# RWKV recurrence on TensorE: output products grouped by their shape, heads alternating in the products within chunks

## The chip, the cores and the metric

The kernel runs on one core of one Trainium2 chip. The metric is the device time of one execution in microseconds; the median of three runs is given. A core has five engines that matter here: TensorE (PE, whose weight loads are listed apart as PEld), VectorE (DVE), ScalarE (ACT), GpSimd (POOL) and SyncE (SP), which issues DMAs. TensorE multiplies a stationary operand (rows x columns of its 128x128 array) with a moving operand and writes into PSUM.

## The reference

Two transformer stacks of two layers each run one after the other on a sequence of 256 tokens of width 1024. The change is inside the first mixer of the second stack, the RWKV-7 recurrence, which has 8 heads of 64 channels:

```python
def step(state, inp):
    r_t, w_t, k_t, v_t, kk_t, a_t = inp
    sa = jnp.einsum('bhij,bhj->bhi', state, -kk_t)
    state = (state * w_t[:, :, None, :] + sa[..., None] * (kk_t * a_t)[:, :, None, :]
             + v_t[..., None] * k_t[:, :, None, :])
    return state, jnp.einsum('bhij,bhj->bhi', state, r_t)
...
_, y = lax.scan(step, state0, (tm(r), tm(decay), tm(k), tm(v), tm(kk), tm(a)))
```

The state of a head is 64x64. Beside the recurrence stands a stick-breaking attention of 8 heads on the same input; the outputs of both go into one product with `w_out`.

## The kernel before

All activations stand transposed, channels on partitions and the 256 tokens along the free side. Weights stream from HBM in 399 chunks of 128x1024 through four raw buffers; ACT makes a high part of a chunk (L418) and DVE a low part (L419), and every product with weights is three matmuls (helper at L385, as are nearly all others, so tiles and not lines tell them apart).

The recurrence is not run token by token. The 256 tokens are four chunks c of 64. The 8 heads are four pairs j, and e says which half of the 128 partitions a head of a pair has. Ahead of the chunks, `gp(j)` makes the products of one pair within all chunks: for each e and c a stationary operand of 64 rows x 128 columns from `BK` and a moving one of 128 columns from `KR`, into one PSUM tile for each e. DVE masks the results into `GR` (what a token's output takes from earlier tokens of its chunk) and `GB`. `am` makes the matrices that `invl`, `invc` and `invs` invert: the matrices go through DRAM (tiles dA, dY, dZ), DVE does 15 short rows of the inversion, and `lw_`, `ly`, `lz` finish it on PE.

Then the chunks follow one another, each with four steps:

- `ck(c)`: from chunk 1 on, 8 products of 64x64 quarters of the array, `KR` with the state `S0`; DVE adds them up (L1314).
- `ct(c)`: 8 products of quarters; ACT and DVE copy them into `SV` (L1321, L1322).
- `cs_(c)`: 8 products of 128 rows x 64 columns; DVE makes the next state `S1` (L1332, L1333).
- `cy(c)`: the output. For each of 8 heads one product of `SV` and `GR` over 128 rows and 64 columns, and, from chunk 1 on, one product of a 64x64 quarter, `S0` with `KR`, that is added to it. All go into one PSUM tile of the pool "o"; ACT copies it out (L1348).

These are float32 products; the trace shows two passes on PE for each, so 8 products stand there as x16. Which step stands where on PE is written out by hand in HYB_ORDER, and PE keeps that order. Between the steps of the chunks it has steps of the attention: `sz` (scores), `sp` (transposes at L783 and products with the values), `gt` (gate), `gn` and `gv` (norm of the output). Around them:

```python
cs_.0 cy.0 jv.1 ck.1 sp.0 ct.1 gt.2 sz.2.0 cs_.1 cy.1 sz.2.1 ck.2 sp.1 ct.2 sz.3.0 gn.0 cs_.2 gt.1 sz.3.1 cy.2
ck.3 sp.2 ct.3 gt.3 gv.0 cy.3 sp.3 gvf.0
```

This is HYB_ORDER from the end of chunk 0 on. The order on DVE, ACT, POOL and SP is not written by hand: a scheduler sets it when the program is built, from the order in which the instructions are written and its own estimate of when each is ready. PSUM tiles come by turns from the pools "s" and "t", two buffers each; "o" has one.

Of the kernel before, what the change touches and what calls it, by code (L numbers as in the profile page):

```python
# [20 lines left out]
P = 128  # L21
# [302 lines left out]
class Net:  # L324
# [685 lines left out]
    def hybrid_body(self, p, X):  # L1010
# [10 lines left out]
        half = lambda e: slice(64 * e, 64 * e + 64)  # L1021
# [24 lines left out]
        for i, x in enumerate((dY, dZ)):  # L1046
            y = x.rearrange("t e a b -> (t e) (a b)")
            for k in range(2):
                nc.sync.dma_start(out=y[:, k * 512:k * 512 + 512], in_=zero)
        SV = one("SV", P, 4, 4, 2, 64)  # L1050
        RW0 = 1536
        R = dict(kx={}, rx={}, vx={}, gl={}, qa={}, kv={}, kr={}, vr={}, ENL={}, TA={}, KP={}, KR={}, BK={}, GR={}, GB={},
                 MA={}, Y={}, Y2={}, Z={}, W={}, G1={}, BG={}, bo={}, BV={}, BT={}, ST={}, YC={}, OB={}, out={}, ps={}, ps2={})
# [117 lines left out]
        def gp(j):  # L1171
            KR, BK = R["KR"][j], R["BK"][j]
            gb = c64(f1())
            gm = lambda o: cst["gmask"][:, o:o + 64].unsqueeze(1).to_broadcast([P, 4, 64])
            for e in range(2):
                ps = self.pa([P, 4, P])
                for c in range(4):
                    self.mm(ps[:, c], BK[half(e), c, e:e + 2], KR[half(e), c])
                gr = self.t(p, [P, 4, 64], "GR", bufs=8)
                v.tensor_tensor(gr, ps[:, :, 64:128], gm(64), ALU.mult)  # L1180
                r2 = half(1 - e)
                v.tensor_tensor(gb[r2], ps[r2, :, 0:64], gm(0)[r2], ALU.mult)
                R["GR"][j, e] = gr
            R["GB"][j] = gb
# [116 lines left out]
        each = [(j, e) for j in range(4) for e in range(2)]  # L1301
# [36 lines left out]
        def cy(c):  # L1338
            if c == 0:
                R["y"] = [b2(2, S) for _ in range(2)]  # L1340
            yps = self.po([P, 4, 64])
            for j, e in each:
                o = yps[half(e), j]
                self.mm(o, SV[:, j, c, e], R["GR"][j, e][:, c], stop=c == 0)
                if c:
                    self.mm(o, R["S0"][half(e), j], R["KR"][j][half(e), c, 1], start=False)
            for q in range(2):
                a.copy(R["y"][q][:, :, c * 64:c * 64 + 64], yps[:, 2 * q:2 * q + 2])  # L1348
            R["S0"] = R["S1"]
# [376 lines left out]
```

## Time and profile before

| | us |
|---|---|
| median of 3 runs | 1318.56 |
| lowest and highest run | 1316.29, 1318.71 |
| profiled execution | 1321.39 |
| its span, first instruction to last | 1319.6 |
| PE busy | 1292.5 (98%) |
| PEld busy | 1231.4 (93%) |
| DVE busy | 1026.5 (78%) |
| ACT busy | 781.9 (59%) |
| steps gp (first to last product) | 626 to 657 |
| chunks 1 to 3, with the steps between them | 703 to 751 |

Busy time of PE is modelled at the end of each matmul, so that a busy PE need not be at its peak; how fast it goes is read from the distance between the starts of two groups of the timeline. A group there is a run of alike instructions: start, length, engine, line, operation, out<-in by the program's names, the part of the array (rows*columns), the moving operand's shape, and how many. Idle time of the engine before a group stands in brackets, with what ended it.

### The profile page before, as it was taken

The page shows a single profiled execution, that of the slowest core. Times are in us where ns is not written, and L with a number is a line of the kernel's source. Part 1 is how long each engine was busy: PE and PEld are TensorE (multiplying, and loading weights), DVE is VectorE, ACT ScalarE, POOL GpSimd, SP SyncE. Part 2 cuts the span into 40 slices and gives each one's busy share as a digit, 9 for nine tenths or more (in the row PEclk, how much of TensorE's full clock was granted, in tenths as well). Part 3 has the DMA queues.
Part 4 walks back from the last instruction along what each step waited for, and adds up shares of the span by engine and source line. Part 5 has one row for each costly group of instructions (what it writes and reads, how often), then busy time and mean ns, then how long its engine had stood idle before and what let it go on. Part 6 is the DMA issues. An engine that isn't in the chain of part 4 may idle for free.

```text
span 1319.6 us, 27125 instructions
## 1 busy us (share of the span) xinstructions
PE 1292.5 (98%) x10864; PEld 1231.4 (93%) x10864; DVE 1026.5 (78%) x2037; ACT 781.9 (59%) x1359; POOL 16.1 (1%) x48
## 2 busy tenths in 40 slices
PE   7999999999999999999999999999999999999997
PEld 5999999988899999999876799999998989999997
DVE  5889997566679998578964488897779978889656
ACT  6667665457667665448343266665557766665544
POOL 0000000000000000001100000000000000000000
PEclk9999999999999999999998799999999999999998
DMA  7566555555446556574440056565555436665551
GB/s 271 176 225 193 189 189 182 189 187 177 132 145 192 191 180 190 191 237 145 124 129 18 17 167 206 192 190 182 189 176 161 127 113 189 193 198 181 191 182 60
DMA packets 70398, 223.18 MB, mean 169 GB/s; under 512 B 13408, under 2 KB 15712, under 8 KB 70272
## 3 DMA queue, kind: packets, MB, share of 16 engines
q1 hardware_dynamic: 63312, 212.43, 50.3%
q10 hardware_dynamic: 6192, 5.34, 1.4%
q0 software_dynamic: 768, 3.67, 0.8%
q8 instruction: 85, 1.39, 0.4%
q14 instruction: 41, 0.34, 0.1%
HBM read 218.53 MB, written 2.88 MB: 168 GB/s over the span
## 4 chain that ended last, share of the span: by engine, by line
PE 92%; DVE 4%; DMA 2%; ACT 1%; issue 1%; SPq 0%; ACTq 0%; DVEq 0%
PE g L385 78%; PE s L385 6%; PE t L385 3%; PE o L385 3%; PE t L783 1%; DVE wlo L419 1%; DMA raw<-in_wall 0%; DMA b<-dZ 0%; DVE tm L1217 0%; ACT whi L418 0%; DMA dA<-b 0%; DVE sqa L171 0%; DVE xl L497 0%; DVE tm L1219 0%; DMA tm<-dA 0%
## 5 line engine op out<-in xcount | busy, mean ns | idle before, releaser
L385 PE MATMUL g<-xh,whi 128*128 128x256 f32 x2184 | 618.0, 283 | 1.4 <-ACT xh L496 1.4
L385 PE MATMUL g<-xl,whi 128*128 128x256 f32 x2184 | 610.3, 279 | 2.5 <-DVE xl L497 2.4
L419 DVE TENSOR_TENSOR wlo<-raw,whi 128x1024 fp32r<-128x1024 f32 (+1 forms) x400 | 487.8, 1221 | 160.4 <-ACT whi L418 157.4
L418 ACT ACTIVATE whi<-raw 128x1024 fp32r<-128x1024 f32 (+1 forms) x400 | 421.9, 1055 | 317.4 <-PE g L385 172.5
L385 PE MATMUL g<-xh,wlo 128*128 128x256 f32 x2184 | 609.6, 279 | 0.1
L385 PEld LDWEIGHTS g<-xh,whi 128*128 128x128 f32 x2184 | 410.7, 188 | 7.2 <-issue 4.0
L385 PEld LDWEIGHTS g<-xl,whi 128*128 128x128 f32 x2184 | 410.9, 188 | 4.0 <-DVE xl L497 3.3
L385 PEld LDWEIGHTS g<-xh,wlo 128*128 128x128 f32 x2184 | 414.1, 190 | 0.3 <-DVE wlo L419 0.3
L385 PE MATMUL g<-hh,wlo 128*128 128x256 f32 x704 | 197.8, 281 | 0.0
L385 PE MATMUL g<-hl,whi 128*128 128x256 f32 x704 | 197.8, 281 | 0.0
L385 PE MATMUL g<-hh,whi 128*128 128x256 f32 x704 | 197.8, 281 | 0.0
L385 PEld LDWEIGHTS g<-hh,wlo 128*128 128x128 f32 x704 | 135.2, 192 | 0.0
L385 PEld LDWEIGHTS g<-hh,whi 128*128 128x128 f32 x704 | 132.2, 188 | 0.0
L385 PEld LDWEIGHTS g<-hl,whi 128*128 128x128 f32 x704 | 132.2, 188 | 0.0
L277 ACT ACTIVATE hh<-pr 128x256 fp32r<-128x256 f32 x88 | 36.0, 409 | 48.7 <-DVE pr L272 48.7
L496 ACT ACTIVATE xh<-h,vec 128x256 fp32r<-128x256 f32 x80 | 39.1, 499 | 24.0 <-DVE h L560 20.9
L867 ACT ACTIVATE c<-pad,vec 128x256 f32<-128x256 f32 x88 | 47.7, 590 | 9.4 <-DVE pad L856 9.4
L874 DVE SCALAR_TENSOR_TENSOR c<-pad,vec,c 128x256 f32<-128x256 f32 x88 | 42.7, 485 | 3.1
L497 DVE SCALAR_TENSOR_TENSOR xl<-h,vec,xh 128x256 fp32r<-128x256 f32 x80 | 37.9, 481 | 6.9 <-ACT xh L496 6.8
L872 DVE SCALAR_TENSOR_TENSOR c<-pad,vec,c 128x256 f32<-128x256 f32 x88 | 42.2, 480 | 0.0
L282 DVE TENSOR_TENSOR hl<-pr,hh 128x256 fp32r<-128x256 f32 x88 | 36.9, 420 | 3.9 <-ACT hh L277 3.9
L385 PE MATMUL g<-whi,xh 128*128 128x512 f32 x68 | 29.1, 428 | 9.2 <-ACT xh L496 9.2
(375 smaller groups left out, 1396.1 us busy)
## 6 DMA issues: line engine op xcount, KB each, us to landing
raw<-in_wall SPq DMA_DIRECT2D x398, 512.0 KB, 3.5
bias<-in_bias POOLq DMA_DIRECT2D x4, 768.0 KB, 7.1
cst_c<-in_c ACTq DMA_DIRECT2D x1, 896.0 KB, 7.1
raw<-in_wall SPq DMA_DIRECT2D x2, 256.0 KB, 4.1
h<-in_x ACTq DMA_DIRECT2D x2, 256.0 KB, 4.3
h<-in_x POOLq DMA_DIRECT2D x2, 256.0 KB, 7.6
ws<-in_ws ACTq DMA_DIRECT2D x1, 512.0 KB, 8.7
bs<-in_bs ACTq DMA_DIRECT2D x1, 512.0 KB, 8.8
```

The lines of the kernel that those rows point to most:

```text
L277: self.net.nc.scalar.activation(self.H[-1][0], self.pr, AF.Copy)
L282: self.net.nc.vector.tensor_tensor(hl, self.pr, hh.bitcast(F32), ALU.subtract)
L385: self.nc.tensor.matmul(out, lhsT=lhsT, rhs=rhs, start=start, stop=stop, skip_group_check=True)
L418: nc.scalar.activation(hi[:, s], raw[:, s], AF.Copy)
L419: self.after(nc.vector.tensor_tensor(lo[:, s], raw[:, s], hi[:, s].bitcast(F32), ALU.subtract))
L496: self.nc.scalar.activation(xh, h, AF.Copy, scale=gain)
L497: self.nc.vector.scalar_tensor_tensor(xl, h, gain, xh.bitcast(F32), ALU.mult, ALU.subtract)
L783: self.nc.tensor.transpose(pt[:, b * P:b * P + P], w[:, s * P:s * P + P], self.cst["ident"])
L867: a.activation(c0, pad[:, j, 2:], AF.Identity, bias=self.col("f_conv_b", (l,), j * KF + i), scale=cw(2, j))
L872: v.scalar_tensor_tensor(c1, pad[:, j, 1:S + 1], cw(1, j), cc[n], ALU.mult, ALU.add)
L874: v.scalar_tensor_tensor(cc[n], pad[:, j, 0:S], cw(0, j), c1, ALU.mult, ALU.add)
```

## The change

Two places of the RWKV step are written in another order. Every product of before is there after, with the same operands and the same size.

In `gp`, both PSUM tiles of a pair are taken first, and within a chunk c the products of both heads e follow one another; before, the four products of one head came first and the four of the other second. The two heads' stationary operands lie in different halves of the array's rows.

In `cy`, the 8 products of 128 rows come first, and then, from chunk 1 on, the 8 quarter products; before, each quarter product stood right behind its head's product of 128 rows. Since only the first write of a bank now carries the start flag, `start` is set for j = 0 alone.

```diff
-            for e in range(2):
-                ps = self.pa([P, 4, P])
-                for c in range(4):
-                    self.mm(ps[:, c], BK[half(e), c, e:e + 2], KR[half(e), c])
+            both = [self.pa([P, 4, P]) for _ in range(2)]
+            for c in range(4):
+                for e in range(2):
+                    self.mm(both[e][:, c], BK[half(e), c, e:e + 2], KR[half(e), c])
+            for e, ps in enumerate(both):
                 gr = self.t(p, [P, 4, 64], "GR", bufs=8)
...
             yps = self.po([P, 4, 64])
+
             for j, e in each:
-                o = yps[half(e), j]
-                self.mm(o, SV[:, j, c, e], R["GR"][j, e][:, c], stop=c == 0)
-                if c:
-                    self.mm(o, R["S0"][half(e), j], R["KR"][j][half(e), c, 1], start=False)
+                self.mm(yps[half(e), j], SV[:, j, c, e], R["GR"][j, e][:, c], start=j == 0, stop=c == 0)
+            for j, e in each if c else ():
+                self.mm(yps[half(e), j], R["S0"][half(e), j], R["KR"][j][half(e), c, 1], start=False)
```

On PE, the output of chunk 1 (`cy.1`) began like this before. GR with SV is a product of 128 rows, b (a `KR`) with tm (the state) a quarter product; the numbers tell tiles apart.

```order
L385 MATMUL s_9614<-SV_7880,BK_9075 64x64 x4
L385 MATMUL o_9627<-GR_8619,SV_7880 64x64
L385 MATMUL o_9627<-b_8453,tm_9532 64x64
L385 MATMUL o_9627<-GR_8627,SV_7880 64x64
L385 MATMUL o_9627<-b_8453,tm_9532 64x64
L385 MATMUL o_9627<-GR_8956,SV_7880 64x64
L385 MATMUL o_9627<-b_8380,tm_9532 64x64
L385 MATMUL o_9627<-GR_8964,SV_7880 64x64
```

The same place of the changed kernel, to its end and to the score products that follow:

```order
L385 MATMUL o_9627<-GR_8624,SV_7880 64x64
L385 MATMUL o_9627<-GR_8627,SV_7880 64x64
L385 MATMUL o_9627<-GR_8961,SV_7880 64x64
L385 MATMUL o_9627<-GR_8964,SV_7880 64x64
L385 MATMUL o_9627<-GR_8729,SV_7880 64x64
L385 MATMUL o_9627<-GR_8732,SV_7880 64x64
L385 MATMUL o_9627<-GR_8779,SV_7880 64x64
L385 MATMUL o_9627<-GR_8782,SV_7880 64x64
L385 MATMUL o_9627<-b_8453,tm_9532 64x64 x2
L385 MATMUL o_9627<-b_8380,tm_9532 64x64 x2
L385 MATMUL o_9627<-b_8549,tm_9532 64x64 x2
L385 MATMUL o_9627<-b_8568,tm_9532 64x64 x2
```

What alternated 15 times between the two shapes is now two runs of 8; `cy.2` and `cy.3` read alike. `cy.0`, which has no quarter products, is as before.

PE at the first of the four `gp` steps: a head's four products follow each other before, and the heads (tiles t and s) alternate now.

```order
 L385 MATMUL g_8468<-xh_7823,wlo_8471 128x256
-L385 MATMUL t_8614<-b_8453,BK_8454 128x128 x4
-L385 MATMUL s_8622<-b_8453,BK_8454 128x128 x4
+L385 MATMUL t_8614<-b_8453,BK_8454 128x128
+L385 MATMUL s_8615<-b_8453,BK_8454 128x128
+L385 MATMUL t_8614<-b_8453,BK_8454 128x128
+L385 MATMUL s_8615<-b_8453,BK_8454 128x128
```

The scheduler also puts a few instructions of DVE and ACT in another order between the `gp` steps and the end of the inversion. DVE at the end of the inversion's 15 rows (the reduction of 128x15 is the last of them; the copy at L1220 makes what goes to dZ), before:

```order
L1219 TENSOR_REDUCE tm_8816<-tm_8818 128x15
L419 TENSOR_TENSOR wlo_8925<-raw_8923,whi_8924 128x1024
L1220 COPY tm_8817<-tm_8816 128x256
L1308 COPY tm_9376<-b_8907 128x128
L1267 TENSOR_TENSOR f_8948<-t_8946,f_8432 128x256
```

and after (lines from `gp` to `cy` have one number more):

```order
L1220 TENSOR_REDUCE tm_8816<-tm_8818 128x15
L1221 COPY tm_8817<-tm_8816 128x256
L1309 COPY tm_9376<-b_8907 128x128
L419 TENSOR_TENSOR wlo_8925<-raw_8923,whi_8924 128x1024
L1268 TENSOR_TENSOR f_8948<-t_8946,f_8432 128x256
```

The low part of a weight chunk moved from before that copy to behind it. POOL and SP have the order of before.

## Rows read from the trace of the kernel before

**Rows 1.** The page, part 2: granted TensorE clock in 40 slices of 33 us, tenths.

```profile
PEclk9999999999999999999998799999999999999998
```

**Rows 2.** The chain of work that ended last, 590 to 770 us: start, us, what.

```profile
709.72 4.10 PE o L385 x32
...
742.71 5.62 PE o L385 x32
```

**Rows 3.** Timeline of PE, cy.0 to the start of cy.1: start, us, instructions.

```profile
701.45 0.64 PE L385 MATMUL o<-GR,SV 128*64 128x64 f32 x16
702.01 1.12 PE L385 MATMUL s<-b,cst_c 128*128 128x512 f32 x2
...
703.07 0.68 PE L385 MATMUL t<-tm,b 64*64 64x64 f32 x16
703.68 0.55 PE L783 MATMUL t<-cst_c,st 128*128 128x128 f32 x3
...
706.32 0.68 PE L385 MATMUL s<-tm,b 64*64 64x64 f32 x16
706.93 1.32 PE L385 MATMUL t<-sg,b 128*128 128x256 f32 x4
708.18 0.92 PE L385 MATMUL s<-f,f 64*128 64x128 f32 x4
709.03 0.69 PE L385 MATMUL s<-SV,BK 128*64 128x64 f32 x16
709.54 0.28 PE L385 MATMUL o<-GR,SV 128*64 128x64 f32 x2
709.75 0.33 PE L385 MATMUL o<-b,tm 64*64 64x64 f32 x2
710.01 0.33 PE L385 MATMUL o<-GR,SV 128*64 128x64 f32 x2
```

**Rows 4.** Timeline of PE, first groups at the ends of cy.1, cy.2 and cy.3.

```profile
713.75 1.64 PE L385 MATMUL s<-f,f 64*128 64x128 f32 x4
715.32 1.12 PE L385 MATMUL t<-tm,b 64*64 64x64 f32 x16
...
728.81 0.33 PE L385 MATMUL o<-GR,SV 128*64 128x64 f32 x2
...
734.13 1.16 PE L385 MATMUL t<-tm,b 64*64 64x64 f32 x15
...
742.64 0.33 PE L385 MATMUL o<-GR,SV 128*64 128x64 f32 x2
...
748.26 1.54 PE L783 MATMUL t<-cst_c,st 128*128 128x128 f32 x6
...
751.43 0.27 PE L1474 MATMUL t<-cst_c,nwy 128*8 128x128 f32 x1
```

**Rows 5.** Stretches: length, busy us of PE, PEld, DVE, ACT, POOL, then PEclk, DMA.

```profile
700.00:713.30 13.30, 13.10 (x138) 8.27 (x136) 7.25 (x21) 4.67 (x11) 0.00 (x0) 1.00 0.01 2
713.40:726.90 13.50, 12.93 (x78) 8.72 (x78) 5.37 (x15) 3.14 (x8) 0.13 (x2) 0.50 0.00 0
```

**Rows 6.** Timeline of PE at gp.0.

```profile
626.44 0.82 PE L385 MATMUL t<-b,BK 64*128 64x128 f32 x5
...
627.21 0.27 PE L385 MATMUL s<-b,BK 64*128 64x128 f32 x1
627.22 0.27 PE L385 MATMUL t<-b,BK 64*128 64x128 f32 x1
...
628.08 0.39 PE L385 MATMUL g<-xh,whi 128*128 128x256 f32 x1
```

**Rows 7.** Stretches again: from gp.0 to the end of the inversion on DVE.

```profile
628.10:654.60 26.50, 26.04 (x275) 22.07 (x274) 24.87 (x66) 11.10 (x20) 3.44 (x4) 1.00 0.46 135
```

**Rows 8.** What PE waited for, 612 to 672 us: in total, times, longest.

```profile
PE t L385 <- DMA b<-dZ: 2.5, 2, 2.0
```

**Rows 9.** Timeline of DVE, ahead of the copy at L1220.

```profile
655.77 1.21 DVE L419 TENSOR_TENSOR wlo<-raw,whi 128x1024 fp32r<-128x1024 f32 x1
```

## The prediction

> **What bounds the kernel now.** I read the page first, then the chain of waits, then the timeline of TensorE, and last the granted clock by stretches. The page's clock line shows the one soft place of the execution: TensorE has its full clock from the second slice to the last but one, except in two or three slices in the middle [rows 1], which is where the chunks of the recurrence run. The chain of work that ended last lies on PE there, and the output products stand in it as whole pieces: 4.10 us for cy.1, 5.62 us for cy.3 [rows 2]. So PE bounds this stretch, and what is taken from PE's work in it is taken from the end, until another engine's result is late.
>
> The timeline shows why these pieces are long. cy.0, which has the 128-row products alone, takes 16 passes in 701.45 to 702.01, 0.56 us, 35 ns a pass. A group of 16 quarter passes (ck.1) takes 703.07 to 703.68, 0.61 us. In cy.1, where the two kinds alternate, the groups of two passes start at 709.54, 709.75 and 710.01: 0.26 us for two passes that take 0.07 us in a group of their kind [rows 3]. Each change of shape so costs about 0.19 us, and there are 15 within a cy.
>
> **The change in cy.** From its first product to the next step's, cy.1 takes 709.54 to 713.75, 4.21 us; cy.2 takes 728.81 to 734.13, 5.32 us; cy.3 takes 742.64 to 748.26, 5.62 us [rows 3, 4]. Together 15.15 us. After, one cy is 0.56 us of 128-row passes, one change of shape at 0.19 us and 0.61 us of quarter passes: 1.36 us at the full clock, 4.08 us for three. That is 11.07 us less, all of it on the path. At half clock I bound a cy by twice that, 2.72 us. cy.0 has nothing to regroup: nothing. The start flag is a bit of the same instruction: nothing.
>
> **What the clock gives back.** The stretch 700 to 713.3 had 1.00 of the clock, 2.4 GHz, and the stretch 713.4 to 726.9 had 0.50, 1.2 GHz [rows 5]: the fall came after 3.8 us in which PE did nothing but alternate. The stretch before holds the same kinds of steps (ck, sp, ct, gt, sz, cs) and kept the full clock, so these steps alone don't lose it. I take it that after the change it stays. Then the steps between the cy cost what their twins cost before the fall, start to start [rows 3]: ck 0.61, sp 2.64 (703.68 to 706.32, its waits for ACT in it), ct 0.61, gt 1.25, sz 0.85, cs 0.51. For gn and gv, which have no twin, I take the largest like group, 1.25. From cy.1 to cy.2 stand three sz, ck, sp, ct, gn, cs and gt: 2.55 + 0.61 + 2.64 + 0.61 + 1.25 + 0.51 + 1.25 = 9.42 us in place of 713.75 to 728.81, 15.06 us [rows 4]: 5.64 less. From cy.2 to cy.3 stand ck, sp, ct, gt and gv: 6.36 in place of 8.51: 2.15 less. sp.3 behind cy.3: 2.64 in place of 748.26 to 751.43, 3.17: 0.53 less. Together 8.32 us; none of it if the clock falls as before.
>
> **Waits that were covered.** Each cy hid work of DVE: the next state S1, the rows of the scores, the norm. The stretch at full clock had DVE busy for 7.25 of 13.3 us [rows 5], so there is room, but ck waits for S1 behind DVE's score work in its queue, and then DVE's sum for ct is late behind that. I put 0.5 us on it, between 0 and the 4 us that a shortened cy no longer covers.
>
> **The change in gp.** 16 passes take 626.44 to 628.08, 1.64 us, and the rows show both heads already running side by side in the middle: an s pass at 627.21 and a t pass at 627.22, 10 ns apart, though all t passes stand ahead of all s passes in the order [rows 6]. With the heads alternating, all pairs can do so; at best the 1.64 us are halved, 0.82 us less for each of four gp. It can cost something too, since the second head's tile must be free before the first head's second product; the s pass of the old order found it free. I count nothing, because from 628.1 to 654.6 DVE is busy for 24.87 of 26.5 us [rows 7] and the way to the inversion leads over DVE and DMAs; PE then waits at its end for the matrices from DRAM, 2.5 us [rows 8], and what PE saves in gp lengthens that wait. If this cover were gone, gp would be worth up to 3.3 us.
>
> **The new order on DVE and ACT.** A wlo of 1.21 us [rows 9] goes from before the copy that makes dZ to behind it. The transfers that PE waits for can then be issued up to 1.2 us earlier; I take 0.6. Other moves there exchange instructions that had room; between 0.5 us either way, nothing taken. Against this stands the longer wait of PE ahead of the inversion's products: up to 3.3 us of gp more. If the clock falls over it, the dense work behind runs at half for a while. I put 0.8 us, between 0 and the half of a stretch like 713.4 to 726.9 (13.5 us [rows 5]), 6.8.
>
> **Sum.** -11.07 - 8.32 + 0.5 - 0.6 + 0.8 = -18.7 us. The profiled execution took 1321.39 us (span 1319.6), 2.8 us more than the median of 1318.56, and its steps need no scaling for that (0.2%). From the median: 1299.9 us.
>
> **A rule weighed.** The quarter groups ck and ct have their two heads in different halves of the rows and one PSUM tile, and take 38 ns a pass [rows 3]. The Trainium skill (TensorEngine Tiling, section Restrictions and Gotchas) says that different row tiles cannot write the same PSUM bank at the same time; the quarter half of the new cy is written so. By it that half would go one head after the other, by an estimate from the page's rule 1.2 us in place of 0.61, and the sum would be 1.8 us smaller. The rows show no such step in ck, which has the same shape and one bank, and I go by them.
>
> **The rivals.**
>
> *The clock falls as before.* Then cy.1 gives 4.21 - 1.36 = 2.85, cy.2 and cy.3 5.32 - 2.72 and 5.62 - 2.72, together 8.4 us, and the rest keeps its half-clock lengths: 1318.56 - 8.4 = 1310.2. With a fall in one of the stretches it is between. For it: the steps between the cy are no dense work, gv above all, and the twin stretch is only 13 us long. Against it: that stretch held the full clock with the same steps, and what stood ahead of each fall was a cy. 0.20, from 1304 to 1310.
>
> *Another engine becomes the bound.* S1, the sums of ck and the scores go through DVE one after another, and the transposes of sp wait for ACT. If each of the three shortened cy leaves PE a wait of 2 us, the time is 1299.9 + 6 = 1306. For it: DVE's chain behind sz is some 3 us long and stands in the queue ahead of the sum of ck. Against it: sp.0 at full clock had only its own waits for ACT, and they are in its 2.64. 0.12, from 1303 to 1308.
>
> *The grouping doesn't pay.* It may be that not the change of shape costs 0.19 us but the quarter product itself, which adds to what another product has written. Then a cy keeps its length: 1318 to 1319. Against it: ck shows quarter products at 38 ns, and in a float32 product the second pass adds to the first at 35 ns. 0.04.
>
> *Slower.* PE's wait ahead of the inversion's products grows from 2.5 to over 5 us by what gp saves; if the clock falls there and stays at half through the dense stretch from 670 to 701 us, that stretch of 31 us takes up to 31 more, and the time is 1299.9 + 31 = 1331. It decides from about 19 us of loss on. The Trainium skill (TensorE: Matmul & The Clock Gate, section Loop structure matters more than you think) says that a long wait for data makes the next matmuls run at the lower level; in this trace the wait of 2.5 us cost no clock. The longest half-clock stretch here is under 14 us, in thin work, which is worth 7 at most. 0.03.
>
> **How the numbers follow.** The forecast, 1297 to 1303, has 0.61. The range must leave out no more than 2 in 10: from 1296 (gp's saving and the earlier DMAs both in the path) to 1309 it takes in the forecast, most of the waits and most of the clock's cases. What this measurement can tell from no change is 0.2%, 2.6 us. Faster by more: all but the last two rivals, 0.93. Within: 0.04. Slower: 0.03.
>
> **What would show it.** In the changed kernel's timeline a cy from 1 on should be two groups, x16 of GR and x16 of quarters, of 0.5 to 0.7 us each. The clock line should have no slice below 9 in the middle, and sp.1 and sp.2 should be near 2.6 us. gp should be near 1 us, with a longer wait for b<-dZ behind it. The prediction is wrong if the quarter group is as slow as the old pairs, if the clock falls between the cy all the same, or if PE shows waits for DVE at ck or ct of over 1 us each.

## The result and the profile after

The changed kernel takes 1301.22 us (median of 4 runs, 1295.16 to 1301.72) against 1318.63 us for the kernel before (4 runs, 1316.29 to 1321.13). The ratio is 0.9871, 95% interval 0.9839 to 0.9904. The prediction, 1299.9 with a range from 1296 to 1309, holds. In two further comparisons the ratio was 0.9909 [0.9874, 0.9944] and 0.9877 [0.9844, 0.991]. The ratios are not quotients of the medians shown, and they leave out the two slow runs, 1321.79 and 1322.84 us, of the 21 of the kernel before in the next section.

The profiled execution took 1295.16 us, its span 1293.4 us. The page of the changed kernel, parts 1 and 2 (busy time by engine; granted clock in 40 slices, which answers [rows 1]):

```profile
PE 1265.5 (98%) x10864; PEld 1210.3 (94%) x10864; DVE 1023.6 (79%) x2037; ACT 783.9 (61%) x1359; POOL 16.1 (1%) x48
...
PEclk9999999999999999999999999999999999999998
```

The soft place in the middle of the clock line is gone. The timeline of PE from cy.1 to the end of sp.3 answers [rows 3, 4] (start, us, instructions; idle time ahead in brackets):

```profile
703.31 0.64 PE L385 MATMUL o<-GR,SV 128*64 128x64 f32 x16
703.88 0.68 PE L385 MATMUL o<-b,tm 64*64 64x64 f32 x16
704.49 0.92 PE L385 MATMUL s<-f,f 64*128 64x128 f32 x4
705.34 0.68 PE L385 MATMUL t<-tm,b 64*64 64x64 f32 x16
705.95 0.55 PE L783 MATMUL t<-cst_c,st 128*128 128x128 f32 x3
...
708.98 0.68 PE L385 MATMUL s<-tm,b 64*64 64x64 f32 x16
...
714.22 0.69 PE L385 MATMUL o<-GR,SV 128*64 128x64 f32 x16
714.83 0.68 PE L385 MATMUL o<-b,tm 64*64 64x64 f32 x16
715.35 0.63 PE L385 MATMUL t<-tm,b 64*64 64x64 f32 x16
...
721.66 0.69 PE L385 MATMUL o<-GR,SV 128*64 128x64 f32 x16
722.27 0.68 PE L385 MATMUL o<-b,tm 64*64 64x64 f32 x16
722.89 0.88 PE L783 MATMUL t<-cst_c,st 128*128 128x128 f32 x6
...
725.18 0.27 PE L1475 MATMUL t<-cst_c,nwy 128*8 128x128 f32 x1
```

Each cy is now two groups of 16 passes. From its first product to the next step, cy.1 takes 703.31 to 704.49, 1.18 us; cy.2 1.13; cy.3 1.23: 3.54 us in place of 15.15. The steps between take 704.49 to 714.22, 9.73 us, in place of 15.06; 715.35 to 721.66, 6.31 in place of 8.51; 722.89 to 725.18, 2.29 in place of 3.17: 8.41 us less. Together 20.0 us. The chain of work that ended last has cy.1 and cy.2 as pieces of 1.08 and 1.23 us, where [rows 2] had cy.1 with 4.10 and cy.3 with 5.62:

```profile
703.48 1.08 PE o L385 x32
...
714.29 1.23 PE o L385 x32
```

By stretches (length, busy us of PE, PEld, DVE, ACT, POOL, then PEclk and DMA) cy.1 to sp.3 kept the full clock throughout, where [rows 5] fell to 0.50 from 713.4 on:

```profile
704.40:725.30 20.90, 19.61 (x226) 13.26 (x223) 16.04 (x51) 8.54 (x24) 0.23 (x3) 1.00 0.01 2
```

PE waited there three times (what for; us in total, times, longest), 1.3 us together:

```profile
PE t L783 <- ACT st L785: 0.6, 1, 0.6
PE t L783 <- DVE tm L1315: 0.5, 1, 0.5
PE o L385 <- ACT st L785: 0.2, 1, 0.2
```

**Where the difference of the two profiles lies.** Three landmarks cut each execution: the first product of gp.0, the first of cy.1, and the first product behind sp.3 (L1474 before, L1475 after).

| us | start to gp.0 | gp.0 to cy.1 | cy.1 to behind sp.3 | from there to the end |
|---|---|---|---|---|
| before | 626.44 | 83.10 | 41.89 | 568.2 |
| after | 620.78 | 82.53 | 21.87 | 568.2 |
| difference | -5.7 | -0.6 | -20.0 | 0.0 |

The 5.7 us ahead of gp.0 lie in code that the change doesn't touch. They come from a stage that runs at two paces in executions of one and the same kernel (last section), and are not the change's. Its own are 20.6 us, and 20.0 of them are cy and what follows it.

### The profile page after: what moved, and what is told of

Read it like the earlier page. It is cut to its first block, busy times and chain, and to the rows that moved or that the text cites. A ratio compares the mean times of both kernels' runs of the same rounds, so it can differ in the third digit from the quotient of the medians.

```text
span 1293.4 us, 27122 instructions
## 1 busy us (share of the span) xinstructions
PE 1265.5 (98%) x10864; PEld 1210.3 (94%) x10864; DVE 1023.6 (79%) x2037; ACT 783.9 (61%) x1359; POOL 16.1 (1%) x48
## 4 chain that ended last, share of the span: by engine, by line
PE 94%; DVE 4%; ACT 1%; issue 1%; DMA 1%; SPq 0%; DVEq 0%; ACTq 0%
PE g L385 81%; PE s L385 6%; PE t L385 4%; PE o L385 2%; DVE wlo L419 1%; PE t L783 1%; DMA raw<-in_wall 1%; ACT whi L418 0%; DVE sqa L171 0%; DVE xl L497 0%; DVE b L1155 0%; DVE f L1183 0%; DVE out L260 0%; DVE GR L1181 0%; DVE h L984 0%
```

## The experiments

### One half of the change alone

The first kernel has the cy of after and the gp of before; the second the reverse; the third is after once more.

> The output products grouped, gp as before; DVE and ACT keep the order of before. Theory (the gain is in the chunks: 11.6 us of shorter cy, 8.4 us of clock that no longer falls between them): 18 to 21 us faster than before, cy.1 to cy.3 at 1.1 to 1.3 us each, clock 1.00 from 700 us to the last output product, and the wait for b<-dZ ahead of the inversion's products still there with 2 to 3 us. Rival (gp or the new order on DVE and ACT carries part of the gain): under 16 us faster.

> gp with alternating heads, the output products as before; DVE and ACT have the changed kernel's order. Theory (gp is covered): within 2 us of before; gp at 1.1 us in place of 1.64, PE waits 2 to 3 us near the third gp for ACT's copies into SV and for DVE, and waits less for b<-dZ; cy at 4 to 5.6 us and the clock falls between them as before. Rival (gp is worth its own 2 us): 2 us faster. Rival (the wait near the third gp brings a fall of the clock that costs more than gp gives): 1 to 2 us slower.

> The changed kernel once more, beside the two halves on one chip. Theory: 17 to 21 us faster than before, and equal to the output products alone within 2 us. In its trace the stretch from the first of the inversion's products to the step behind cy.3 should again be near 62 us, and the stages ahead of the recurrence may differ by some us from the first trace, since nothing there was changed.

| | median us (runs) | ratio to before, 95% | cy.1 to behind sp.3 | gp.0 to cy.1 |
|---|---|---|---|---|
| before | 1313.47 (21) | | | |
| cy alone | 1298.81 (6) | 0.9899 [0.9855, 0.9942] | 21.87 | 82.43 |
| gp alone | 1315.64 (12) | 1.0029 [1.0003, 1.0055] | 34.36 | 82.57 |
| after again | 1300.39 (7) | 0.9909 [0.9874, 0.9944] | 21.87 | 82.49 |

cy alone gives the whole gain. gp alone gives none; by its interval it costs 0.03 to 0.55%, of which 82.57 against 83.10 in the gp stage shows nothing. The gains were smaller than expected: 14.7 us by the medians for cy alone (18 to 21 expected) and 13.1 for after (17 to 21). The rival of the first text, under 16 us because gp carries part of the gain, is met in its number but not in its cause, since after, which has the new gp too, gained no more than cy alone.

In this comparison the gain was some 4 us smaller than at first. The likely reason is that the kernel before has no fixed time. With the alternating cy, the gp-alone kernel has its clock falls elsewhere (725.6 to 732.4 us, from within cy.2, and 739.2 to 746.1, from within cy.3; none behind cy.1), so that cy.1 to behind sp.3 took 34.36 us and not the 41.89 of the first profile. Its three cy took 4.06, 5.15 and 4.61 us (the last two in part at half clock); of the 12.5 us that it lies above after's 21.87, 10.3 are these and 2.2 the slow clock in the steps between and behind them, where the first profile had 8.4. Runs of before spread alike: 1301.14 us with a mean granted clock of 0.992, 1317.31 us with 0.982.

### One cy back: is the fall of the clock the cy's?

After, with cy.1 alone alternating as before:

```diff
+            n = 1 if c == 1 else 8
+            for i in range(0, 8, n):
+                for j, e in each[i:i + n]:
+                    self.mm(yps[half(e), j], SV[:, j, c, e], R["GR"][j, e][:, c], start=j == 0, stop=c == 0)
+                for j, e in each[i:i + n] if c else ():
+                    self.mm(yps[half(e), j], R["S0"][half(e), j], R["KR"][j][half(e), c, 1], start=False)
```

> The changed kernel with cy.1 alone alternating again head by head; cy.2 and cy.3 stay grouped. Theory (an alternating cy makes the clock fall and the steps behind it pay): cy.1 at 4.2 us, the clock falls to half at its end, and the steps between cy.1 and cy.2 take 12 to 15 us in place of 9.7; 5 to 9 us more than the changed kernel from the start of cy.1 to the end of cy.3. Rival (the clock falls there by chance or by the thin steps themselves): only the 3 us of cy.1, and 9.7 us between.

It took 1304.3 us in one run (before: 1312.45). Its timeline of PE and its stretches:

```profile
704.43 0.28 PE L385 MATMUL o<-GR,SV 128*64 128x64 f32 x2
704.64 0.32 PE L385 MATMUL o<-b,tm 64*64 64x64 f32 x2
...
708.49 1.64 PE L385 MATMUL s<-f,f 64*128 64x128 f32 x4
```

```profile
704.40:708.50 4.10, 4.10 (x41) 3.02 (x36) 2.93 (x8) 0.11 (x1) 0.00 (x0) 0.99 0.01 4
708.50:722.00 13.50, 12.93 (x77) 8.55 (x76) 5.73 (x17) 3.13 (x8) 0.13 (x2) 0.50 0.00 0
```

The cy takes 4.07 us (704.43 to 708.49), and right at its end the clock falls to 1.2 GHz for 13.5 us, as in [rows 5]. The same steps up to cy.2 then take 15.23 us in place of 9.73. cy.1 to behind sp.3 takes 30.25 us against 21.87: 8.4 more, 2.9 of them the cy itself and 5.5 what the clock takes behind it. So the alternating cy is enough to bring the fall. That it always does isn't so: in the gp-alone kernel cy.1 alternates just so (4.06 us) and the clock holds until cy.2. Over all profiles: four have cy that alternate between two shapes (before, gp alone, this one, and the one that is called not adjacent below), ten such cy in all, and eight of them have a fall that begins inside them, 0.6 to 4.0 us after their first product. In the ten profiles without such a cy the clock stays at 2.4 GHz from cy.1 to behind sp.3.

### Larger groups, one shape, no neighbours: what in the alternation costs

Three theories for the 0.19 us that the prediction puts on a change: the change of shape; the quarter product's adding to what the product just ahead has written; the quarter products themselves. The first kernel has groups of 2 heads in cy.1 and of 4 in cy.2 (`n = (8, 2, 4, 8)[c]` in the loop above). The second keeps the alternating order of before, but takes the quarter product over all 128 rows, so that both kinds have one shape. The third alternates, but each quarter product belongs to the head before (GR0 GR1 q0 GR2 q1 ...).

```diff
-                    self.mm(yps[half(e), j], R["S0"][half(e), j], R["KR"][j][half(e), c, 1], start=False)
+                    self.mm(yps[half(e), j], R["S0"][:, j], R["KR"][j][:, c, 1], start=False)
```

> The changed kernel with cy.1 in groups of 2 heads and cy.2 in groups of 4; cy.3 stays in groups of 8. Theory (a change of shape costs a fixed time; the groups of 1 and of 8 heads give 0.022 us for a pass and 0.24 us for a change): a group of 2 heads takes 3 x 0.022 + 0.24 = 0.30 us, eight of them 2.4 us for cy.1; a group of 4 heads takes 0.39 us, four of them 1.6 us for cy.2; cy.3 1.2 us. Rival (the cost lies with a product that adds to what the one just before it has written, so that any grouping removes it): 1.2 us for all three.

> The changed kernel with the products of cy alternating head by head as before, but the second one taken over all 128 rows in place of the 64 of its head. It so adds the other head's part too: the output of chunks 1 to 3 is another one. Every product still adds to what the one before it has written, and no product changes the shape. Theory (the shape): cy.1 to cy.3 at 1.1 to 1.3 us. Rival (the adding to what was just written): 4.1 us and more.

> The changed kernel with shapes alternating in cy, but each quarter product one head late, so that it never adds to what the product before it has written; 13 changes of shape in place of 15 of before and 1 of the changed kernel. Theory (the shape): 12 x 0.26 and two pairs of 0.30, 3.7 us for cy.1, longer at half clock for the others. Rival (the adding to what was just written): 1.2 to 1.5 us.

They took 1301.13, 1296.06 and 1314.76 us in one run each, and from cy.1 to behind sp.3 23.04, 21.72 and 34.19 us. The timelines of PE in groups of 2 heads, and with one shape:

```profile
709.09 0.29 PE L385 MATMUL o<-GR,SV 128*64 128x64 f32 x4
709.30 0.33 PE L385 MATMUL o<-b,tm 64*64 64x64 f32 x4
709.56 0.34 PE L385 MATMUL o<-GR,SV 128*64 128x64 f32 x4
709.83 0.33 PE L385 MATMUL o<-b,tm 64*64 64x64 f32 x4
...
711.14 0.92 PE L385 MATMUL s<-f,f 64*128 64x128 f32 x4
```

```profile
705.35 0.33 PE L385 MATMUL o<-GR,SV 128*64 128x64 f32 x4
705.46 0.34 PE L385 MATMUL o<-b,tm 128*64 128x64 f32 x4
705.58 0.33 PE L385 MATMUL o<-GR,SV 128*64 128x64 f32 x4
...
706.43 0.92 PE L385 MATMUL s<-f,f 64*128 64x128 f32 x4
```

With one shape an alternating cy takes 1.08 us (cy.2 and cy.3: 1.13), 4 passes in 0.116 us, 29 ns each: alternation costs nothing where the shape stays. Not adjacent, the cy take 3.56, 4.17 and 5.29 us, near the old lengths: adjacency is not it. Nor are the quarter products themselves, since 16 of their passes take 0.61 us in after's cy.1. The change of shape is.

| cy at full clock | changes of shape, those at its two ends included | us |
|---|---|---|
| one head by turns (cy.1 of the one-cy-back kernel) | 16 | 4.07 |
| groups of 2 heads | 8 | 2.06 |
| groups of 4 heads (cy.2: a change ahead of it, none behind) | 4 | 1.42 |
| grouped (after, cy.1) | 2 | 1.18 |
| one shape (cy.1) | 1 | 1.08 |

What does one change cost? In groups of 2, 4 and 8 heads the distance from a group's start to the next is 0.26, 0.38 and 0.61 us, of which the passes at 29 ns are 0.12, 0.23 and 0.46: the change costs 0.15 us, whatever the size of the group. I had expected 2.4 and 1.6 us for the two cy, with one price of some 0.2 us for every change.

A group of a single head takes 0.26 us too, as long as a group of 2 heads with twice the passes. The first passes of cy.1 show why, after (703.30 to 703.36 us) and before (709.53 to 709.60):

```profile
703.31 0.23 PE L385 MATMUL o<-GR,SV 128*64 128x64 f32 x2
```

```profile
709.54 0.22 PE L385 MATMUL o<-GR,SV 128*64 128x64 f32 x1
```

Within some 60 ns two passes have started grouped, and one where the head stands alone. By the single starts in the traces, grouped passes come in pairs: the second 7 ns behind the first, the next pair 58 ns after the first one. A head alone starts its second pass only after 58 ns. So a pair is a pass of each of two heads side by side, and products that alternate head by head between the shapes never have a neighbour of their own shape to pair with. Passes without a partner take 0.116 us for a head, and with 0.15 us for the change that is the 0.26 measured. By this reckoning some 2.1 of the 2.89 us that grouping saves in a cy are changes (14 at 0.15 us), and the rest are the partners. With one shape the passes pair too, though heads and kinds alternate as before.

### The wait behind the third gp

In after, PE waits for 2.6 us behind the third gp, and the clock falls there; the kernel before waits 0.4 us there and keeps its clock. (The gp run in the order 0, 2, 3, 1 of HYB_ORDER, so the third is gp.3. The expectations below count them in order of time and call it gp.2.) What PE waited for at 612 to 668 us, to be read with [rows 8], and the stretch of the fall:

```profile
PE t L385 <- ACT SV L1264: 1.9, 1, 1.9
PE s L385 <- DVE f L1183: 0.7, 1, 0.7
PE t L385 <- DVE f L1183: 0.2, 1, 0.2
```

```profile
638.10:641.30 3.20, 3.20 (x23) 2.14 (x21) 2.25 (x12) 0.00 (x0) 0.00 (x0) 0.50 0.46 187
```

The timeline of all engines there. ACTq is a DMA issue on ACT's queue, SV a copy of what the step behind the gp has transposed:

```profile
632.92 1.21 DVE L419 TENSOR_TENSOR wlo<-raw,whi 128x1024 fp32r<-128x1024 f32 x1
...
634.00 1.00 ACTq L1211 DMA_DIRECT2D tm<-dA  x2
...
634.38 1.21 DVE L419 TENSOR_TENSOR wlo<-raw,whi 128x1024 fp32r<-128x1024 f32 x1
...
635.04 0.37 ACT L1263 COPY SV<-t 64x256 f32<-64x256 f32 x1 [2.48 <-issue]
635.42 0.36 ACT L1264 COPY SV<-t 64x256 f32<-64x256 f32 x1
635.51 0.41 DVE L1181 TENSOR_TENSOR GR<-t,cst_c 128x256 f32<-128x256 f32 x1
...
635.84 0.68 PE L385 MATMUL t<-cst_c,f 64*64 64x64 f32 x16 [1.93 <-ACT SV L1264]
...
637.18 0.70 PE L385 MATMUL s<-f,cst_c 128*128 128x256 f32 x2 [0.66 <-DVE f L1183]
```

The same place before, where the masks are L1180 and L1182:

```profile
638.55 1.21 DVE L419 TENSOR_TENSOR wlo<-raw,whi 128x1024 fp32r<-128x1024 f32 x1
...
640.01 0.41 DVE L1180 TENSOR_TENSOR GR<-t,cst_c 128x256 f32<-128x256 f32 x1
...
641.01 0.68 PE L385 MATMUL t<-cst_c,f 64*64 64x64 f32 x16 [0.37 <-DVE f L1182]
...
641.57 1.21 DVE L419 TENSOR_TENSOR wlo<-raw,whi 128x1024 fp32r<-128x1024 f32 x1
```

Two suspects stand in it: ACT's copy SV behind two DMA issues that take 1.00 us (they stand ahead of it before, too), and DVE's masks of the third gp (L1181, L1183) behind two low parts of 1.21 us, where the order of before has only one ahead of them. The first was tried by putting all four reads of dA on SP:

```diff
-                (nc.sync, a)[tb % 2].dma_start(out=R["inv"][0][tb * 32:tb * 32 + 32], in_=blk(dA, tb))
+                nc.sync.dma_start(out=R["inv"][0][tb * 32:tb * 32 + 32], in_=blk(dA, tb))
```

> The changed kernel, with the four reads of dA (the blocks to be inverted) all issued by SP; in the changed kernel ACT issues two of them, and its copies into SV stand behind the issue, which waits for dA to land. Theory (this queue holds PE near the third gp): the wait of 1.9 us for SV and the fall of the clock at that place go, and the kernel is 1 to 3 us faster than the changed one. Rival (DVE's chain and the DMAs set the time there, as for gp): PE waits as long a little later, no difference within 1 us. Rival (SP's queue of weight loads stands behind the reads): 1 to 3 us slower.

1300.56 us (9 runs), 0.9893 [0.9857, 0.993], no other than after on the same chip. The wait for SV shrank to 0.2 us, and 2.4 us for DVE's mask f (L1183) and 1.1 for dZ took its place; the clock fell all the same (642.8 to 646.2 us), and gp.0 to cy.1 took 84.11 us. ACT's queue was the last to hold PE there in after, not the only one.

The second suspect needs the order of before on DVE with less than its PE time. Two orders of the products differ by two exchanges of neighbours on PE: t t t s t s s s keeps the masks ahead of the second low part, t t s t s t s s has after's order on DVE. After and the cy-alone kernel ran on the same chip.

```diff
-            for c in range(4):
-                for e in range(2):
-                    self.mm(both[e][:, c], BK[half(e), c, e:e + 2], KR[half(e), c])
+            for c, e in ((0, 0), (1, 0), (2, 0), (0, 1), (3, 0), (1, 1), (2, 1), (3, 1)):
+                self.mm(both[e][:, c], BK[half(e), c, e:e + 2], KR[half(e), c])
```

> The changed kernel with the products of a gp in the order t t t s t s s s in place of t s t s t s t s; the cy are those of the changed kernel. The point of this order: VectorE's instructions behind gp.2 stand as in the kernel before (the masks L1180 and L1182 ahead of the second low part wlo), while PE's passes are nearer to the changed kernel. Theory V (the order on VectorE makes PE's wait behind gp.2 and the fall of the clock there): no wait for SV, no fall of the clock between 630 and 650 us, gp.0 to cy.1 near the 82.4 us of the kernel with the old gp. Theory P (what PE saves in gp makes them): a wait for SV of 1 us or more and a fall of the clock near 640 us, 82.5 to 85 us. A gp should take 1.2 to 1.5 us from its first product to the next step by both. The median by either: 1293 to 1303 us.

> As the run before, with the order t t s t s t s s: one product of each head is exchanged on PE, and VectorE has the order of the changed kernel there (the second low part wlo ahead of the masks). Theory V: the wait for SV of some 2 us and the fall of the clock near 640 us are back. Theory P: the same as in the run before to within 0.5 us of waits, and a fall in both or in none. gp 1.1 to 1.4 us. The median: 1293 to 1303 us.

> The cy of the changed kernel with the gp of the kernel before, once more, on the same chip as the two runs before. If the alternating of the heads in gp is worth something in the end, this is slower than the changed kernel by up to 3 us; if its wait and its fall of the clock cost more than it saves, faster by 1 to 2 us; no fall of the clock near 640 us. I expect no difference above 1.5 us between runs of the same level of the stage ahead of gp.

> The changed kernel once more, on the same chip, to be compared with the three runs before. A fall of the clock near 640 us and a wait for SV of 1.8 to 2.0 us; cy.1 to gvf 21.9 us; median 1295 to 1302 us.

What PE waited for with t t t s t s s s, and with t t s t s t s s:

```profile
PE t L385 <- DVE f L1182: 1.1, 1, 1.1
PE t L385 <- DMA b<-dZ: 0.7, 1, 0.7
```

```profile
PE t L385 <- ACT SV L1263: 2.5, 1, 2.5
```

| gp, cy grouped in all | one gp, us | PE waits, us | half clock behind the third gp | gp.0 to cy.1 | median us (runs) | ratio to before, 95% |
|---|---|---|---|---|---|---|
| of before | 1.64 | 1.5 | none | 82.31 | 1293.44 (4) | 0.9834 [0.9805, 0.9863] |
| t t t s t s s s | 1.42 | 1.8 | none | 81.62 | 1295.8 (4) | 0.9851 [0.9805, 0.9898] |
| t t s t s t s s | 1.19 | 2.5 | 634.9 to 638.3 | 82.73 | 1294.1 (4) | 0.9844 [0.9814, 0.9874] |
| alternating (after) | 1.09 | 2.7 | 644.6 to 648.0 | 82.63 | 1300.5 (4) | 0.9877 [0.9844, 0.991] |

The wait for SV and the fall come with the order on DVE. Between the two middle rows a gp differs by 0.23 us; the wait for SV goes from none to 2.5 us, and the stretch is 1.1 us longer although its PE steps are shorter. ACT has the same order in both up to this place and differs only behind it. All fourteen profiles agree on the fall: the ten with after's order on DVE have one of 3.4 or 6.8 us behind the third gp, the four with the order of before there (before, twice cy alone, and t t t s t s s s) have none.

So the scheduler's new order, a by-product, goes with the fall, and a shorter gp alone didn't bring it (1.42 us in place of 1.64). Two things stay open. PE's waits in all (1.5, 1.8, 2.5, 2.7 us) also rise as a gp gets shorter, so that a part of them may be what PE saves. And the order isn't all that moved: in after PE writes the tile it waited for at 635.84, behind ACT's copies and ahead of the mask at 635.94, so it has the buffer that the copies free; before, it writes it at 641.01, ahead of the copies (641.43), in the buffer that the masks free. As for the size, the lengths of this stretch spread: the kernels of after's gp with other cy took 82.57 to 85.09 us for gp.0 to cy.1, so 1.1 us between two single traces are no firm price. None of them, nor after itself (82.49 to 82.63), is below the 82.31 and 82.43 of cy alone.

The medians don't resolve these kernels: the 7 us between after and cy alone here stand ahead of the change, where gp.0 starts at 627.20 and 619.70 us. A version that clearly beats after has not been found; t t t s t s s s is the shortest in the stretch, by one trace.

## Why the prediction was right, point by point

- **cy at 1.36 us each, 11.07 us less**: right in mechanism, a little small in size. The cy take 1.18, 1.13 and 1.23, and 11.61 us are gone. The mis-sized term is the change of shape: the two group lengths, 0.56 and 0.61 us, were read from start to the next start and so already hold the change at their end; the 0.19 us were added once too often. The 0.19 itself was a change (0.15 us) and the missing partner in one, which doesn't alter the forecast.
- **The clock gives back 8.32 us**: 8.41 measured, and the clock stayed full. By stretches it was 5.33, 2.20 and 0.88 against 5.64, 2.15 and 0.53. The twins fitted in sum; the bound 1.25 us for gn and gv was too large (1.06 and 0.98 us), sp.1 with 3.03 us and sp.2 with 2.90 lie above the 2.64 that were taken, and sp.3 with 2.29 below. That the stretch [rows 5] was a fair twin was the choice that decided 8 us, and putting one cy back confirms it from the other side: one alternating cy costs 5.5 us behind itself. But the size is that of one execution; with the falls elsewhere the clock's share was 2.2 us.
- **Waits that were covered, 0.5 us**: 1.3 us in all, 0.6 of them for ACT's st in sp.1, where the kernel before waited as long (0.57 us, at half clock). The prediction read sp.0's 2.64 us as holding its waits for ACT; the trace has one wait there, 0.20 us for DVE's tm (L1314). New are 0.5 us for that tm (now L1315) in sp.2 and 0.2 for st in sp.3. DVE was busy for 16.04 of 20.9 us. The rival *another engine becomes the bound* doesn't hold.
- **gp counts for nothing**: right in the sum, wrong in the place. A gp takes 1.09 us (the second 1.50), 0.55 less than before, of the 0.82 that were put as its best. Each pass of one head starts with one of the other, to be read with [rows 6]:

```profile
631.51 0.37 PE L385 MATMUL t<-b,BK 64*128 64x128 f32 x1
631.52 0.37 PE L385 MATMUL s<-b,BK 64*128 64x128 f32 x1
```

  But the wait for b<-dZ [rows 8] didn't grow; it is gone in all three profiles of after. The time went into the wait for SV behind the third gp, a place that the prediction doesn't name, with a half clock of 3.4 us behind it. The step that failed is "Other moves there exchange instructions that had room": the second low part ahead of the third gp's masks had none.
- **The earlier dZ, -0.6, and the longer wait with its clock, +0.8**: together 0.2 us of loss were taken, and 0.6 of gain were measured against the one profile of before; against cy alone (82.43 and 82.31 us) the gp part of after (82.49 to 82.63) is no gain at all.
- **The rule weighed**: the quarter half of a cy takes 0.61, 0.52 and 0.62 us, and its two heads start 7 ns apart; they didn't go one after the other, and no part of the 1.8 us that the prediction kept apart appeared. The Trainium skill (TensorEngine Tiling (Array Packing), section Restrictions and Gotchas) says that row tiles can't use one PSUM bank at the same time; as a price in time, this trace doesn't show it.
- **The rivals**: *the clock falls as before* didn't happen in any of the eight profiles with all cy grouped in their two kinds. *The grouping doesn't pay* falls with the 0.52 to 0.62 us of a quarter group. *Slower* had half of its condition in all three profiles of after: the clock fell in this stage, for 3.4 us and not 31, but behind the third gp and not behind a longer wait for dZ.

The median, 1301.2, is nearer to 1299.9 than the terms deserve. The change's own part in the two profiles is 20.6 us, and 1318.6 less that would be 1298; but how much before loses to the clock and how fast the stage ahead of gp runs differ from run to run by more than that distance. That the median came so close is luck.

## What to carry to other kernels

Small matmuls of two shapes shouldn't alternate: group them by their shape, and price a change from the starts in the timeline, here 0.15 us against passes of 29 ns. Within one shape the opposite holds: products in different parts of the array may alternate, and where they did, two heads ran side by side (gp, 1.09 in place of 1.64 us). Look then at the granted clock behind such a place, since the steps that follow may pay more than the place itself, and count that share as one that differs from run to run. Where a scheduler sets other engines' order, read that order again even for an edit that only swaps products: here a low part of 1.21 us moved ahead of a mask, the clock fell behind it, and nothing was left of what the swap gave.

## What the runs showed of the hardware

**Passes of two heads start out of the program's order.** In [rows 6] an s pass starts at 627.21 us, ahead of t passes that stand before it. The heads use different halves of the array's rows. The Trainium skill (TensorE: Matmul & The Clock Gate, Part 3: Packing small matmuls, The mechanism) says that matmuls start and end in program order without reordering; by the starts of this trace they don't between the two row halves. The measurement decides here, with the reserve that ends are modelled.

**A stage of dense work has two paces at the full clock.** The feed-forward stage ahead of the recurrence has the same 1352 matmuls in 159.0 us in the profile of before and in 153.0 in that of after:

```profile
408.00:567.00 159.00, 159.00 (x1352) 159.00 (x1351) 134.65 (x213) 95.96 (x148) 0.46 (x7) 1.00 0.59 189
```

```profile
408.00:561.00 153.00, 153.00 (x1352) 153.00 (x1351) 132.15 (x213) 98.36 (x148) 0.46 (x7) 1.00 0.61 196
```

That is some 0.118 and 0.113 us from one start to the next, both with a granted clock of 1.00 and with no idle time on PE. Both paces occur with the same kernel, as the start of gp.0 behind this stage shows: after started gp.0 at 620.78, 626.62 and 627.20 us in three executions, cy alone at 620.31 and 619.70. These 6 us are a third of what the change gives. What sets the pace is open.
